# Feed-forward buffers of a streaming encoder layer at other starting addresses

## The chip, the cores and the metric

The kernel runs on one core of one Trainium2 chip. The metric is the device time of one execution in microseconds; the kernel before takes 2368.96 us, the median of three runs (2368.94 to 2370.51 us). A smaller time is better. All data is float32; the products run on TensorE in the fp32r form, each value split beforehand into a high and a low part.

## The reference, cut to what matters

One layer of an encoder is computed for a prompt of 2048 tokens and for 8 short samples of 16 tokens each, with `d_model` 1024. Written per token, with the states of the recurrent part left out:

```
q, k, v, gates, qa, ka, va = split(x @ w_in)            # 1024 -> 2824
hm = og * head_norm(mlstm(q, k, v, gates))              # 4 heads x 128
ha = swa(rope(qa), rope(ka), va)                        # 8 heads x 64
h  = layer_norm(alpha * x + concat(hm, ha) @ w_out)
u  = h @ w_up                                           # 1024 -> 2 * 2816
c  = b_conv + sum(ext(u)[j:j+T] * w_conv[j], j=0..2)    # over time, causal
a, g = split(c)
y  = layer_norm(alpha * h + (silu(g) * a) @ w_down)     # 2816 -> 1024
```

The outputs are `y` for the prompt and the samples, and the states that the next step needs. The change touches the lower half alone, the feed-forward (`w_up`, convolution, gate, `w_down`), and the end of the output projection by one pool.

## The kernel before, in words

Everything is done once, in stages that follow each other on TensorE without a pause: the input projection with the recurrent part and the attention woven into it, the output projection with its layer norm, the up-projection (`f_ups`), the down-projection (`f_downs`). The order of TensorE's instructions is that in which the program writes them; the tile framework adds the semaphores and lays out the memory.

The up-projection works in three blocks of tokens (`FBLOCKS`: 6, 6 and 5 tiles of 128 tokens). A block's normalised rows are transposed on TensorE into `hraw`, with the model dimension on the partitions. Products follow a seven-product scheme of Strassen's kind: for each of the 22 pairs of feature tiles `j`, seven sums of feature quarters (numbers `s` = 1 to 7) are multiplied with seven sums of weight quarters. A sum of features is split into a high part `hh` and a low part `hl` (`f_tokens`, `split` at L217 and L218), once per block; a sum of weights is split into one buffer `uw`, high half and low half one behind the other (`f_next`). One product `(b, j, s)` is twelve matmuls (`f_product`, L1831): four slices of the contraction, and for each of them high by high, high by low, low by high:

```
for k in range(4):
    for i, (l, r) in enumerate(((wh, hh), (wh, hl), (wl, hh))):
        mm(ps, l[:, k], r[:, k], ...)
```

The first operand `l`, here the weights, is loaded into the array (the stationary operand, a LDWEIGHTS in the profile); the second, `r`, here the features, is streamed through it (the moving operand, 384 columns in blocks 0 and 1, 320 in block 2). That is 22 x 7 x 12 = 1848 matmuls in each block. In the profile's rows the moving operand stands first: `dps<-hh,uw` is a product that writes the PSUM tile `dps`, streams `hh` and has `uw` loaded.

The down-projection uses the same scheme with the roles exchanged (L2034): the gated features `fu`, split into the six buffers that held `hh1` to `hl6`, are stationary, and the weights `uw` stream through, 512 columns at a time, in 1980 matmuls.

The output projection before them (`group`, by `mm3` at L222 to L224) also streams 512 columns of weights (`w`) past stationary features (`oh`, `ol`).

Memory is handed out by pools, which are stacks. A pool gives each tag its place in the order in which the tags first come; every tile takes its size rounded up to 32 bytes of a partition. A pool on the left begins where the one below it ends, and one on the right ends at the top and so begins lower when it gets larger. The starting addresses of the buffers in the program before, in bytes of a partition:

| buffers | pool | start | remainder by 256 |
|---|---|---|---|
| `uw`, `w`: 8 weight buffers, 4096 bytes in slots of 4224 | `wsb` | 17088 + 4224 i, 50368 + 4224 i | 192 and 64 in turn |
| `uw`: two spare weight buffers | `wx2sb` | 67584, 71680 | 0 |
| `w`: two spare weight buffers of the output projection | `wx1sb` | 141312, 145408 | 0 |
| `oh`, `ol` | `xsb` | 75776 + 4096 i | 0 |
| `hh`, `hl` of `s` = 2, 5, 3 | `f2sb` | 75776 + 6144 i | 0 |
| `hh`, `hl` of `s` = 4; `cc`, `th` | `f3sb` | 127520 and on | 32 |
| `hraw`, `hh` and `hl` of `s` = 1, 7, 6, all `fu` | `fsb` | 159712 and on | 224 |

The slices that a matmul reads lie whole multiples of 512 bytes behind these starts, so that the remainder by 256 of a buffer is that of each of its slices. The ten weight buffers `uw` are taken in turn (`f_slot`, `self.slot` modulo 10: eight of `wsb`, then two of `wx2sb`). The weights for a product are begun six to eight products ahead of it (`AHEAD`).

## Time and profile before

| what | value |
|---|---|
| median of three runs | 2368.96 us |
| span of the profiled execution (first to last instruction) | 2366.3 us |
| what lies around the span, against the median | 2.66 us |
| TensorE busy | 2318.5 us, 98% |
| VectorE, ScalarE, GpSimd busy | 77%, 54%, 12% |
| mean granted TensorE clock | 0.994 |
| TensorE's matmuls of the up-projection | 937.6 to 1881.2 us |
| TensorE's matmuls of the down-projection | 1883.1 to 2358 us |

The profiled execution's own time is its span and the time around it; the profile gives the span alone, and the median is 2.66 us above it. A matmul's row shows how long one was under way (0.34 us for 384 columns), but matmuls follow one another before the last has ended; what a matmul costs the program is the distance from its start to the next one's start, which is called its pitch from here on.

### The profile page before, as it was taken

The page shows a single profiled execution, that of the slowest core. Times are in us where ns is not written, and L with a number is a line of the kernel's source. Part 1 is how long each engine was busy: PE and PEld are TensorE (multiplying, and loading weights), DVE is VectorE, ACT ScalarE, POOL GpSimd, SP SyncE. Part 2 cuts the span into 40 slices and gives each one's busy share as a digit, 9 for nine tenths or more (in the row PEclk, how much of TensorE's full clock was granted, in tenths as well). Part 3 has the DMA queues.
Part 4 walks back from the last instruction along what each step waited for, and adds up shares of the span by engine and source line. Part 5 has one row for each costly group of instructions (what it writes and reads, how often), then busy time and mean ns, then how long its engine had stood idle before and what let it go on. Part 6 is the DMA issues. An engine that isn't in the chain of part 4 may idle for free.

```text
span 2366.3 us, 39878 instructions
## 1 busy us (share of the span) xinstructions
PE 2318.5 (98%) x14425; PEld 2122.9 (90%) x14425; DVE 1828.0 (77%) x3180; ACT 1282.8 (54%) x2423; POOL 281.7 (12%) x322
## 2 busy tenths in 40 slices
PE   8999999999999999999999999999999999999998
PEld 8999998998987777999999999999999978778776
DVE  8677587796689888987888776778766786895987
ACT  5353466776765565555556455555544544444543
POOL 0101101101112121200000000002100100300400
PEclk8999999999999999999999999999999999999999
DMA  7788889889976667787777899878998776657753
GB/s 276 268 302 298 289 284 324 282 288 328 301 256 224 228 208 254 279 309 281 280 270 254 308 310 318 307 247 291 320 276 258 218 280 218 232 175 222 229 167 107
DMA packets 296933, 624.98 MB, mean 264 GB/s; under 512 B 47004, under 2 KB 140192, under 8 KB 296736
## 3 DMA queue, kind: packets, MB, share of 16 engines
q1 hardware_dynamic: 294144, 612.99, 76.5%
q0 software_dynamic: 1728, 6.29, 0.7%
q10 hardware_dynamic: 864, 3.15, 0.4%
q8 instruction: 114, 1.87, 0.3%
q14 instruction: 83, 0.68, 0.1%
HBM read 451.78 MB, written 170.56 MB: 263 GB/s over the span
## 4 chain that ended last, share of the span: by engine, by line
PE 67%; DVE 9%; issue 4%; ACT 2%; DMA 2%; POOL 1%; SPq 0%; DVEq 0%; POOLq 0%; ACTq 0%
PE dps L1831 18%; PE fup L1831 18%; PE fht L2034 5%; PE dps L2034 5%; PE dps L700 5%; PE fup L2034 4%; PE dps L222 2%; PE dps L224 2%; PE dps L223 2%; PE ppo L1337 1%; DVE uw L218 1%; DVE w L218 1%; PE psc L1288 1%; PE dps L726 1%; DVE hl L218 1%
## 5 line engine op out<-in xcount | busy, mean ns | idle before, releaser
L1831 PE MATMUL dps<-hh,uw 128*128 128x384 f32 (+1 forms) x1848 | 481.3, 329 | 6.7 <-ACT u L1856 1.9
L1831 PE MATMUL fup<-hh,uw 128*128 128x384 f32 (+1 forms) x1848 | 480.3, 328 | 2.4 <-ACT u L1856 2.2
L1831 PEld LDWEIGHTS dps<-hh,uw 128*128 128x128 f32 x1848 | 330.0, 188 | 10.2 <-ACT u L1856 2.7
L1879 DVE SCALAR_TENSOR_TENSOR cc<-u,cw,cc 128x768 f32<-128x768 f32 (+1 forms) x264 | 252.4, 977 | 107.2 <-ACT cc L1877 105.3
L1831 PEld LDWEIGHTS fup<-hh,uw 128*128 128x128 f32 x1848 | 330.2, 188 | 3.7 <-ACT u L1856 3.1
L1831 PE MATMUL fup<-hl,uw 128*128 128x384 f32 (+1 forms) x924 | 302.9, 328 | 1.7 <-DVE hl L218 1.7
L1831 PE MATMUL dps<-hl,uw 128*128 128x384 f32 (+1 forms) x924 | 302.5, 327 | 0.0
L700 PE MATMUL dps<-w,oh 128*128 128x256 f32 x1344 | 257.9, 286 | 3.4 <-ACT zev L767 1.9
L218 DVE TENSOR_TENSOR w<-wraw,w 128x1024 fp32r<-128x1024 f32 (+2 forms) x167 | 190.5, 1148 | 60.7 <-ACT w L217 60.0
L217 ACT CAST w<-wraw 128x1024 fp32r<-128x1024 f32 (+2 forms) x167 | 163.1, 986 | 124.4 <-PE dps L700 49.4
L217 ACT CAST uw<-wraw 128x1024 fp32r<-128x1024 f32 x126 | 122.9, 977 | 195.7 <-PE dps L2034 99.3
L700 PEld LDWEIGHTS dps<-w,oh 128*128 128x128 f32 x1344 | 212.9, 190 | 15.6 <-issue 8.9
L218 DVE TENSOR_TENSOR uw<-wraw,uw 128x1024 fp32r<-128x1024 f32 x126 | 150.6, 1197 | 62.6 <-ACT uw L217 62.4
L1877 ACT ACTIVATE cc<-u,cw 128x768 f32<-128x768 f32 (+1 forms) x132 | 129.6, 998 | 117.2 <-DVE u L1870 59.5
L700 PE MATMUL dps<-w,ol 128*128 128x256 f32 x672 | 188.9, 281 | 0.0
L2034 PE MATMUL fup<-uw,fu 128*128 128x512 f32 x726 | 176.6, 399 | 9.4 <-ACT fht L2041 6.9
L2034 PEld LDWEIGHTS fup<-uw,fu 128*128 128x128 f32 x726 | 136.9, 189 | 44.4 <-ACT fht L2041 7.8
L1831 PEld LDWEIGHTS fup<-hl,uw 128*128 128x128 f32 x924 | 173.5, 188 | 2.5 <-DVE hl L218 2.5
L700 PE MATMUL dps<-oh,w 128*128 128x256 f32 x896 | 169.4, 284 | 5.9 <-ACT dps L775 2.8
L1831 PEld LDWEIGHTS dps<-hl,uw 128*128 128x128 f32 x924 | 173.6, 188 | 0.0
L2034 PE MATMUL dps<-uw,fu 128*128 128x512 f32 x660 | 165.0, 395 | 0.0
L700 PEld LDWEIGHTS dps<-oh,w 128*128 128x128 f32 x896 | 141.4, 190 | 12.2 <-issue 4.1
(328 smaller groups left out, 4661.3 us busy)
## 6 DMA issues: line engine op xcount, KB each, us to landing
uw<-zw SPq DMA_DIRECT2D x176, 512.0 KB, 4.7
zw<-uw SPq DMA_DIRECT2D x88, 512.0 KB, 3.0
w<-zws SPq DMA_DIRECT2D x72, 512.0 KB, 6.4
wv<-wup SPq DMA_DIRECT2D x66, 512.0 KB, 5.8
wraw<-wi SPq DMA_DIRECT2D x65, 512.0 KB, 5.2
wraw<-zt SPq DMA_DIRECT2D x60, 512.0 KB, 4.3
wraw<-wdn SPq DMA_DIRECT2D x45, 512.0 KB, 4.0
wraw<-wo SPq DMA_DIRECT2D x40, 512.0 KB, 4.7
```

Source lines behind the costliest of these rows:

```text
L217: nc.scalar.copy(hi, src)
L218: nc.vector.tensor_sub(lo, src, hi.bitcast(F32))
L222: mm(out, ah, bh, start=start, stop=False)
L223: mm(out, ah, bl, start=False, stop=False)
L224: mm(out, al, bh, start=False, stop=stop)
L700: mm(o, l, r, start=s in (1, 7) and c == k == i == 0, stop=k == 3 and i == 2, skip_group_check=True)
L726: mm(o, x, w, start=k == i == 0, stop=k == KD - 1 and i == 2, skip_group_check=True)
L1288: nc.tensor.matmul(ps[kvh][:, j, :nk], q[rs, j0 + j], k[rs, sel], start=i == 0, stop=i == 2)
L1831: mm(ps, l[:, k], r[:, k], start=s in (1, 7) and k == 0 and i == 0, stop=k == 3 and i == 2, skip_group_check=True)
L1877: S.activation(c[:, v], u[:, v, 2:2 + n], AF.Identity, bias=w[3], scale=w[2])
L1879: V.scalar_tensor_tensor(c[:, v], u[:, v, i:i + n], w[i], c[:, v], op0=ALU.mult, op1=ALU.add)
L2034: mm(ps, l[:, k, c], r[:, k], start=s in (1, 4, 7) and u == 0 and k == 0 and i == 0, stop=u == nu - 1 and k == n - 1 and i == 2, skip_grou ...
```

## The change: the buffers' starts

A helper `skew(pool, n)` takes a tile of `n` bytes that nothing reads or writes. It is called at five places:

- 480 bytes at the end of `fsb`, a pool on the right: all of its buffers move 480 bytes down, and `hraw`, `hh`, `hl` of `s` = 1, 7, 6 and `fu` have the remainder 0 by 256 (159232 for `hraw`).
- 64 bytes at the start of `wx1sb` and of `wx2sb`: the spare weight buffers have the remainder 64; `osb` behind `wx1sb` moves by 64 too.
- 448 bytes at the end of `wx2sb`: with the 64 it moves `f2sb`, and later `dsb`, by 512, so that their remainders stay.
- 480 bytes at the end of `f2sb`: `f3sb` moves by 992, from 121888 to 122880, and `hh`, `hl` of `s` = 4, `cc` and `th` have the remainder 0.

The buffers of `wsb`, `xsb` and the input stage stay. No instruction is added, removed or moved.

```diff
+    def skew(self, pool, n):
+        pool.tile([P, n // 4], F32, name="skew", tag=f"skew{n}", bufs=1)
+
...
             wx, wxcm = enter("wx1sb")
+            self.skew(wx, 64)
             self.unit_more(wx)
...
             self.wx, wxcm = enter("wx2sb")
+            self.skew(self.wx, 64)
             self.f2, f2cm = enter("f2sb")
             self.f3, f3cm = enter("f3sb")
             self.f_ups(n)
+            self.skew(self.f2, 480)
+            self.skew(self.wx, 448)
             close(f3cm)
...
             ln2.append(t)
+        self.skew(self.fp, 480)
         self.in_down = True
```

## The prediction, before the result was known

> **What bounds the kernel now.** I read the page's first parts, then the waits of TensorE, the chain of work that ended last, and last the single matmuls in order of time. From the page:

> ```profile
> span 2366.3 us, 39878 instructions
> PE 2318.5 (98%) x14425; PEld 2122.9 (90%) x14425; DVE 1828.0 (77%) x3180; ACT 1282.8 (54%) x2423; POOL 281.7 (12%) x322
> ...
> uw<-zw SPq DMA_DIRECT2D x176, 512.0 KB, 4.7
> ```

> TensorE is the bound. What it waited for from the start of the up-projection to the end (columns: total us, times, longest):

> ```profile
> PE fup L2034 <- ACT fht L2041: 6.9, 2, 3.5
> PE fup L1831 <- ACT u L1856: 2.2, 3, 1.1
> ...
> PE fht L2034 <- DVE yacc L2063: 0.2, 1, 0.2
> ```

> The list has eleven rows, 19.8 us in all; none names a DMA. So in the 1430 us that the change touches nothing but the pitch of the matmuls carries time. The chain of waits (start, length, count) gives it directly, as its pieces there are runs of matmuls that wait for nothing:

> ```profile
> 1020.38 6.25 PE dps L1831 x36
> 1217.77 6.32 PE fup L1831 x36
> 1796.04 5.29 PE dps L1831 x36
> 2265.01 15.40 PE dps L2034 x66
> 2345.47 6.31 PE fht L2034 x27
> ```

> That is 173.6 and 175.6 ns for 384 columns, 146.9 for 320, and 233.3 and 233.7 for 512. Two runs of the same 36 instructions in the up-projection differ by 2 ns a matmul, and neither has a wait in it. Since the instructions are alike, I looked at which buffers they read.

> **Does the pitch depend on addresses?** The timeline of TensorE shows it product by product. The rows below are the first low-part matmul of ten products in turn (all of 384 columns), so that two neighbours lie twelve matmuls apart:

> ```profile
> 1159.11 0.34 PE L1831 MATMUL fup<-hl,uw 128*128 128x384 f32 x1
> 1161.23 0.34 PE L1831 MATMUL fup<-hl,uw 128*128 128x384 f32 x1
> 1163.31 0.34 PE L1831 MATMUL fup<-hl,uw 128*128 128x384 f32 x1
> 1165.40 0.34 PE L1831 MATMUL dps<-hl,uw 128*128 128x384 f32 x1
> 1167.49 0.33 PE L1831 MATMUL fup<-hl,uw 128*128 128x384 f32 x1
> 1169.58 0.34 PE L1831 MATMUL dps<-hl,uw 128*128 128x384 f32 x1
> 1171.67 0.34 PE L1831 MATMUL fup<-hl,uw 128*128 128x384 f32 x1
> 1173.79 0.34 PE L1831 MATMUL dps<-hl,uw 128*128 128x384 f32 x1
> 1175.88 0.34 PE L1831 MATMUL dps<-hl,uw 128*128 128x384 f32 x1
> 1177.95 0.34 PE L1831 MATMUL dps<-hl,uw 128*128 128x384 f32 x1
> ```

> By the order in the code these are `s` = 6, 2, 5 of j = 14, `s` = 1 of j = 15, 3, 7, 4, then 6, 2, 5 of j = 15. Write a product as (remainder by 256 of the streamed features, of the loaded weights). Then (224, 192), the first, takes 2.12 us; (0, 192) 2.08; (0, 64), (224, 64), (0, 64), (224, 64) 2.09 each; (32, 0) 2.12; (224, 0) 2.09; (0, 192) 2.07. So 172.5 to 176.7 ns a matmul, and the same pair gives the same time.

> Over all starts of a stage I sorted the pitches by the pair (streamed operand, operand that is loaded next), leaving out matmuls beside other work and those that hold a wait (here a pitch above 200 ns; 173, 253 and 147 ns for the 320, 512 and 256 columns below). The up-projection's stretch of 384 columns has 3696 matmuls, of which 3628 stay; first and last row:

> ```profile
> 937.61 0.43 PE L1831 MATMUL fup<-hh,uw 128*128 128x384 f32 x1
> ...
> 1607.99 0.34 PE L1831 MATMUL dps<-hh,uw 128*128 128x384 f32 x1
> ```

> Mean pitch in ns (count): (0, 0) 174.91 (302); (0, 64) 174.85 (617); (0, 192) 173.15 (625); (224, 0) 174.22 (305); (224, 64) 174.39 (615); (224, 192) 176.40 (639); (32, 0) 176.78 (107); (32, 64) 174.17 (213); (32, 192) 176.40 (205). The standard errors are 0.07 to 0.21 ns. Products take the weight buffers in turn, so a pair isn't tied to one `s` or one minute of the run.

> **The change part by part.** No instruction, DMA or queue entry goes, comes or moves; every term is a count of matmuls by a difference of pitches.

> *Up-projection, `s` = 1, 7, 6 in blocks 0 and 1* (3 x 44 x 12 = 1584 matmuls): features from 224 to 0, spare weights from 0 to 64. Weighted by the counts, the three cells of 224 average 175.18 ns. Afterwards (0, 64) holds the 920 of the first two and (0, 192) the 639 of the third: 174.15. The price of those pairs is measured, since `s` = 2, 5, 3 have them already. 1.03 ns x 1584 = 1.6 us less.

> *`s` = 4* (528 matmuls): from 32 to 0: 175.57 to 174.19, 0.7 us less. *`s` = 2, 5, 3*: only (0, 0) becomes (0, 64), nothing.

> *Block 2, 320 columns* (1848 matmuls):

> ```profile
> 1598.47 0.31 PE L1831 MATMUL fup<-hh,uw 128*128 128x320 f32 x1
> ...
> 1881.20 0.31 PE L1831 MATMUL dps<-hh,uw 128*128 128x320 f32 x1
> ```

> All nine pairs lie between 146.45 and 146.94 ns; the same sum gives 0.2 us less. Up-projection together: 2.6 us less.

> *Down-projection* (1980 matmuls): the stationary features go from 224 to 0, a fifth of the streamed weights from 0 to 64. First and last row, and 233.28 ns is the mean of 1958 pitches:

> ```profile
> 1883.05 0.95 PE L2034 MATMUL fup<-uw,fu 128*128 128x512 f32 x3
> ...
> 2356.73 1.33 PE L2034 MATMUL fht<-uw,fu 128*128 128x512 f32 x5
> ```

> Now: (0, 224) 232.60 (393), (64, 224) 234.11 (785), (192, 224) 232.80 (780). The pairs that come, (64, 0) for 60% and (192, 0) for 40%, aren't in this stage. They are in the output projection, which streams 512 columns from the same weight buffers past features with the remainder 0:

> ```profile
> 651.04 0.40 PE L222 MATMUL dps<-w,oh 128*128 128x512 f32 x1
> ...
> 928.06 0.39 PE L223 MATMUL dps<-w,oh 128*128 128x512 f32 x1
> ...
> 936.33 0.39 PE L223 MATMUL dps<-w,oh 128*128 128x512 f32 x1
> ```

> Its last 36 matmuls take 8.27 us from the second row to the third, 229.7 ns each. Over the stage, with 816 matmuls, 669 pitches lie between 200 and 260 ns: (0, 0) 230.16 (134), (64, 0) 230.58 (276), (192, 0) 232.58 (259). 0.6 x 230.58 + 0.4 x 232.58 = 231.38: 1.90 ns below 233.28, times 1980 is 3.8 us less. Bounds: at best all of it falls to that stage's best pair, 230.16, which is 6.2 us less. At worst, the input projection's cells, same weight pairs at 256 columns: 3360 matmuls from

> ```profile
> 21.69 0.28 PE L700 MATMUL dps<-oh,w 128*128 128x256 f32 x1
> ...
> 642.80 0.28 PE L700 MATMUL dps<-w,oh 128*128 128x256 f32 x1
> ```

> There (64, 0) is 117.87 (921) and (192, 0) 116.04 (915), mean 116.96; doubled for 512 columns 233.9, 0.6 above today's, 1.2 us more. I take 3.8, by the rows of equal width and equal pairs.

> *Output projection*: its two spare buffers go from (0, 0) to (64, 0); a fifth of 816 by 0.42 is 0.1 us more.

> *VectorE and ScalarE* read and write the moved buffers. I cost this at nothing:

> ```profile
> L218 DVE TENSOR_TENSOR uw<-wv,uw 128x512 fp32r<-128x512 f32 x132 | 90.6, 686 | 49.7 <-ACT uw L217 49.6
> ```

> By weight buffer the means of this group are 685.7 to 686.5 ns for the five remainders by 512, and TensorE covers them: without cover a whole split of 0.69 us is at stake once, not a part of it. *DMAs*: the spare buffers' loads land in 4.7 us (the page's row above) and are issued at least six products of 2.1 us ahead, 12.6 us; they would have to more than double before TensorE waits. *New overlaps in memory*: `hl2`, `hl5`, `hl3` and the second spare buffer reach into one more old buffer of the output projection each. TensorE waits there today, for `hl2`:

> ```profile
> 941.66 0.68 DVE L1608 SCALAR_TENSOR_TENSOR ymix<-ymix,dps 128x512 f32<-128x512 f32 x1
> ...
> 944.06 1.75 DVE L218 TENSOR_TENSOR hl<-hraw,hh 128x1536 fp32r<-128x1536 f32 x1
> ...
> 945.87 0.44 PE L1831 MATMUL fup<-hl,uw 128*128 128x384 f32 x1 [1.51 <-DVE hl L218]
> ```

> L1608 is the last reader of the old buffers, on VectorE itself, and ends at 942.34, before `hl2` is begun in the same queue; so nothing is added. If ScalarE, which waits for the same reader, were held longer by one of its casts, the 1.5 us could about double.

> Sum: 2.6 + 3.8 - 0.1 = 6.3 us less. Against the profiled execution, span 2366.3 to 2360.0; the median of the runs lies 2.66 us above the span, 2368.96 to 2362.7, which is 0.27%. With the bounds of the down-projection, 2360.2 to 2367.7.

> [...]

> **The rivals.**

> 1. *The up-projection alone gains.* The output projection's lower pitch could come from its surroundings instead (VectorE and ScalarE do other things there), and the down-projection stays at 233.3. For it: the input projection's 233.9. Against: equal width and weights in the output projection. 2368.96 - 2.6 = 2366.4.
> 2. *Addresses only look like the cause*, no pitch changes: 2369.0. For it: block 2 shows no dependence at all. Against: the repeated times of equal pairs.
> 3. *Slower: a streamed start at 64 or 192 past stationary features at 0.* In the input projection these cells lie 2.21 ns above the cells with the roles exchanged, (0, 64) 114.51 (604) and (0, 192) 114.99 (614). If that came on top in the down-projection, twice for twice the columns, 4.4 ns x 1980 is 8.7 us more, less the 2.6: 2375.1. It decides from a pitch of 237.0 ns (2.6 + 4.7 us over 1980) in the down-projection. Against: the output projection's (64, 0) and (192, 0), both below 232.6.

> **How the numbers follow.** The forecast has 0.57, rival 1 0.24, rival 2 0.10, rival 3 0.07, and 0.02 is left for more than the best bound. A measurement of this kernel tells about 0.2%, 4.7 us, from no change. A small part of the forecast's share ends above 2364.2 and counts as the same: faster 0.55, same 0.37, slower 0.08. The range takes the best bound and some 0.7 us for the runs' spread below, and rival 2 above: 2359.5 to 2369.6; it leaves out rival 3 and the edges. The likeliest case alone has 2360.2 to 2365.

> **What the changed profile would show.** Chain pieces of 66 matmuls of the down-projection 15.27 us long rather than 15.40; products of `s` = 6 on weights at 192 at 2.08 us rather than 2.12; triples of 36 in blocks 0 and 1 none above 6.29; block 2 still 5.28; the output projection as before; VectorE's and ScalarE's groups and TensorE's list of waits unchanged. The prediction is wrong if the down-projection's pitch stays at 233 or rises, if products on buffers with the remainder 0 differ from today's, or if TensorE's waits grow, at the stage's first products above all.

## The result

The changed kernel takes 2364.59 us, the median of 15 runs (2360.43 to 2370.63), beside 2369.82 us of the kernel before in as many runs on the same chip (2363.58 to 2375.79). The ratio is 0.9976, with a 95% interval of 0.9969 to 0.9983: 0.24% faster, where 0.27% was forecast (2362.7 us; the time lies inside the range). Measured once more on another chip the ratio was 0.9973 (0.9962 to 0.9983; 2364.70 us in 8 runs beside 2371.31 in 24).

The head of the page after the change, with the product groups of the down-projection:

```profile
span 2361.2 us, 39878 instructions
PE 2312.4 (98%) x14425; PEld 2121.3 (90%) x14425; DVE 1829.6 (77%) x3180; ACT 1282.7 (54%) x2423; POOL 268.9 (11%) x322
...
L2042 PE MATMUL fup<-uw,fu 128*128 128x512 f32 x726 | 176.2, 399 | 10.6 <-ACT fht L2049 7.4
...
L2042 PE MATMUL dps<-uw,fu 128*128 128x512 f32 x660 | 163.2, 393 | 0.0
uw<-zw SPq DMA_DIRECT2D x176, 512.0 KB, 4.6
```

The counts of instructions are those of before. The lines have moved (L1831 to L1838, L2034 to L2042, L217 and L218 to L220 and L221, L2041 to L2049, L2063 to L2071). VectorE's and ScalarE's busy times stayed within 1.6 us, and TensorE's fell by 6.1 us. The profiled execution took 2362.99 us with a span of 2361.2, so 1.8 us lie around it.

The pieces of the chain of waits (start, length, count), which answer to those quoted of before:

```profile
958.88 6.45 PE dps L1838 x36
...
1201.17 6.29 PE dps L1838 x36
...
1793.40 5.28 PE dps L1838 x36
...
2260.81 15.22 PE dps L2042 x66
2276.03 14.56 PE fht L2042 x63
2314.11 15.26 PE dps L2042 x66
```

The same 66 matmuls of the down-projection took 15.40 us before and take 15.22 to 15.26 now; 63 took 14.71 and take 14.56. In the up-projection the pieces of 36 that reached 6.31 to 6.36 are gone, and block 2 is at 5.28 as it was. The first piece (6.45; 6.48 before) had been overlooked in the prediction's "none above 6.29": it is the longest in both kernels, whatever the addresses.

Over all matmuls, sorted as in the prediction (mean pitch in ns, by the remainders of the streamed operand and of the one that is loaded next):

| stage | before | pairs now | after | forecast |
|---|---|---|---|---|
| up-projection, 384 columns (3696) | 174.81 | (0, 64) 174.69, (0, 192) 173.25 | 174.10 | 174.85 and 173.15 for the two pairs |
| up-projection, 320 columns (1848) | 146.72 | (0, 64), (0, 192) | 146.56 | 0.1 lower |
| down-projection, 512 columns (1980) | 233.28 | (64, 0) 229.49, (192, 0) 232.54 | 230.71 | 231.38, from 230.58 and 232.58 |
| output projection, 512 columns (816) | 231.27 | (64, 0) 230.32, (192, 0) 232.40 | 231.13 | 0.1 higher |

Count times pitch falls from 917.2 to 914.4 us in the up-projection and from 461.9 to 456.8 us in the down-projection, 7.9 us together. TensorE's waits in the down-projection (total us, times, longest), first those of before that stand behind the 6.9 us for `fht`, then those of after:

```profile
PE fup L2034 <- DVE uw L218: 1.6, 1, 1.6
PE fup L2034 <- DVE yacc L2063: 0.9, 2, 0.5
PE fht L2034 <- DVE yacc L2063: 0.2, 1, 0.2
```

```profile
PE fup L2042 <- ACT fht L2049: 7.4, 2, 3.7
PE fup L2042 <- DVE uw L221: 1.7, 1, 1.7
PE fup L2042 <- DVE yacc L2071: 1.5, 2, 0.8
PE fht L2042 <- DVE yacc L2071: 0.2, 1, 0.2
```

Together they grew from 9.6 to 10.8 us. One stretch shows how: from the start behind a wait for `yacc` to the start behind the next wait for `fht` it is 24.03 us in both kernels (2050.19 to 2074.22 us before, 2046.01 to 2070.04 now). The 87 matmuls between them take 0.24 us less, and the wait behind them is 0.24 us longer (3.71 after 3.47). In the repeat of the changed kernel on another chip the waits add to 10.7 us.

### The profile page after: what moved, and what is told of

Read it like the earlier page. It is cut to its first block, busy times and chain, and to the rows that moved or that the text cites. A ratio compares the mean times of both kernels' runs of the same rounds, so it can differ in the third digit from the quotient of the medians.

```text
span 2361.2 us, 39878 instructions
## 1 busy us (share of the span) xinstructions
PE 2312.4 (98%) x14425; PEld 2121.3 (90%) x14425; DVE 1829.6 (77%) x3180; ACT 1282.7 (54%) x2423; POOL 268.9 (11%) x322
## 3 DMA queue, kind: packets, MB, share of 16 engines
q0 software_dynamic: 1728, 6.29, 0.8%
## 4 chain that ended last, share of the span: by engine, by line
PE 62%; DVE 13%; DMA 5%; ACT 4%; issue 3%; POOL 1%; SPq 0%; DVEq 0%; ACTq 0%; POOLq 0%
PE dps L1838 15%; PE fup L1838 15%; PE dps L707 7%; PE fht L2042 5%; PE dps L2042 5%; PE fup L2042 3%; DMA zf<-cc 2%; DVE cc L1886 2%; PE dps L225 1%; DVE uw L221 1%; PE dps L227 1%; PE dps L226 1%; PE ppo L1344 1%; ACT cc L1884 1%; DVE w L221 1%
## 5 line engine op out<-in xcount | busy, mean ns | idle before, releaser
L1838 PE MATMUL dps<-hh,uw 128*128 128x384 f32 (+1 forms) x1848 | 480.5, 328 | 7.0 <-ACT u L1863 1.9
L1838 PE MATMUL fup<-hh,uw 128*128 128x384 f32 (+1 forms) x1848 | 479.1, 328 | 2.7 <-ACT u L1863 2.5
L1838 PEld LDWEIGHTS dps<-hh,uw 128*128 128x128 f32 x1848 | 329.7, 188 | 11.0 <-ACT u L1863 3.1
L1838 PEld LDWEIGHTS fup<-hh,uw 128*128 128x128 f32 x1848 | 329.8, 188 | 3.9 <-ACT u L1863 3.4
L1838 PE MATMUL fup<-hl,uw 128*128 128x384 f32 (+1 forms) x924 | 302.3, 327 | 0.2 <-DVE hl L221 0.2
L1838 PE MATMUL dps<-hl,uw 128*128 128x384 f32 (+1 forms) x924 | 302.0, 327 | 0.0
L221 DVE TENSOR_TENSOR w<-wraw,w 128x1024 fp32r<-128x1024 f32 (+2 forms) x167 | 190.4, 1148 | 57.0 <-ACT w L220 54.6
L220 ACT CAST w<-wraw 128x1024 fp32r<-128x1024 f32 (+2 forms) x167 | 163.0, 985 | 124.0 <-PE dps L707 44.0
L220 ACT CAST uw<-wraw 128x1024 fp32r<-128x1024 f32 x126 | 122.8, 977 | 192.3 <-PE dps L2042 97.4
L221 DVE TENSOR_TENSOR uw<-wraw,uw 128x1024 fp32r<-128x1024 f32 x126 | 150.6, 1197 | 60.0 <-ACT uw L220 59.5
L2042 PE MATMUL fup<-uw,fu 128*128 128x512 f32 x726 | 176.2, 399 | 10.6 <-ACT fht L2049 7.4
L2042 PEld LDWEIGHTS fup<-uw,fu 128*128 128x128 f32 x726 | 138.0, 191 | 44.1 <-ACT fht L2049 8.2
L1838 PEld LDWEIGHTS fup<-hl,uw 128*128 128x128 f32 x924 | 173.4, 188 | 1.0 <-DVE hl L221 1.0
L1838 PEld LDWEIGHTS dps<-hl,uw 128*128 128x128 f32 x924 | 173.4, 188 | 0.0
L2042 PE MATMUL dps<-uw,fu 128*128 128x512 f32 x660 | 163.2, 393 | 0.0
L707 PEld LDWEIGHTS dps<-oh,w 128*128 128x128 f32 x896 | 141.7, 191 | 13.6 <-issue 4.1
## 6 DMA issues: line engine op xcount, KB each, us to landing
uw<-zw SPq DMA_DIRECT2D x176, 512.0 KB, 4.6
zw<-uw SPq DMA_DIRECT2D x88, 512.0 KB, 2.9
w<-zws SPq DMA_DIRECT2D x72, 512.0 KB, 6.2
wv<-wup SPq DMA_DIRECT2D x66, 512.0 KB, 5.6
wraw<-wi SPq DMA_DIRECT2D x65, 512.0 KB, 5.5
wraw<-zt SPq DMA_DIRECT2D x60, 512.0 KB, 4.3
wraw<-wdn SPq DMA_DIRECT2D x45, 512.0 KB, 4.1
wraw<-wo SPq DMA_DIRECT2D x40, 512.0 KB, 4.9
```

What stands on the lines that cost most here:

```text
L220: nc.scalar.copy(hi, src)
L221: nc.vector.tensor_sub(lo, src, hi.bitcast(F32))
L707: mm(o, l, r, start=s in (1, 7) and c == k == i == 0, stop=k == 3 and i == 2, skip_group_check=True)
L1838: mm(ps, l[:, k], r[:, k], start=s in (1, 7) and k == 0 and i == 0, stop=k == 3 and i == 2, skip_group_check=True)
L2042: mm(ps, l[:, k, c], r[:, k], start=s in (1, 4, 7) and u == 0 and k == 0 and i == 0, stop=u == nu - 1 and k == n - 1 and i == 2, skip_grou ...
```

## The experiments

The theory: what a matmul costs depends on where its streamed operand and the loaded operand begin, and the pitches of the pairs carry the gain. The main rival: the addresses only go along with something else (the work beside it, the order, the block), and any of the new layouts could have brought the same.

**Every pair of remainders, with nothing beside it.** TensorE alone runs series of 24 matmuls from two big tiles, for all 64 pairs of starts in steps of 32 bytes and for four widths:

```
for n in (384, 512, 256, 320):
    for r in range(0, 256, 32):          # start of the streamed operand
        for q in range(0, 256, 32):      # start of the loaded operand
            for i in range(24):
                mm(ps[:, :n], view(sta, q, ...), view(mov, r, ...), ...)
```

> This kernel leaves the whole computation out and writes zeros; TensorE alone runs 24 matmuls for each of 8 x 8 pairs of remainders by 256 bytes (streamed operand, loaded operand) in steps of 32 bytes, at 384, 512, 256 and 320 columns, with no other engine or DMA beside it for most of the time; behind them stand series in which two remainders of the loaded operand alternate. Address theory: the pitch depends on the pair as in the large kernel, at 384 columns (0, 192) near 173.2 ns, (0, 64) near 174.7, (224, 192) and (32, 0) near 176.5; at 512 columns (64, 0) near 229.5, (192, 0) near 232.5, (64, 224) near 234.1; at 320 all pairs within 0.5 ns. In the alternating series the pitch follows the remainder that is loaded next. Rival (the surroundings: other engines' reads and writes at the same time make the differences): no difference over 0.5 ns between the pairs of one width.

Five of its stretches at 512 columns, as a table of windows (window and its length, then busy time and count for TensorE, its weight load, VectorE and GpSimd, the granted clock, DMA share, GB/s). Each reaches from the first start of a pair to that of the next; 24 matmuls start inside, and the count takes in one or two that overlap the edge:

```profile
304.25:309.70 5.45, 5.45 (x25) 4.51 (x25) 0.00 (x0) 0.00 (x0) 1.00 0.00 0
315.30:320.90 5.60, 5.60 (x26) 4.51 (x24) 0.00 (x0) 0.00 (x0) 1.00 0.00 0
337.71:343.21 5.50, 5.50 (x25) 4.51 (x24) 0.00 (x0) 0.00 (x0) 1.00 0.00 0
393.40:398.90 5.50, 5.50 (x25) 4.51 (x24) 0.00 (x0) 0.00 (x0) 1.00 0.00 0
571.57:577.16 5.59, 5.59 (x25) 4.49 (x24) 0.00 (x0) 0.00 (x0) 1.00 0.00 0
```

They are (0, 0), (0, 64), (0, 192), (64, 0) and (192, 0). The granted clock is 1.00 in each, no other engine works, the instruction is the same, and still 24 matmuls take 5.45 to 5.60 us. (0, 192) equals (64, 0), and (0, 64) equals (192, 0): over the whole table, a few cells aside, the pitch follows the difference of the two starts by 256. Typical pitches in ns by that difference (streamed minus loaded):

| columns | 0 | 32 | 64 | 96 | 128 | 160 | 192 | 224 |
|---|---|---|---|---|---|---|---|---|
| 384 | 173.8 | 176.6 | 173.3 | 176.6 | 176.2 | 173.3 | 174.7 | 173.3 |
| 512 | 226.7 | 233.3 | 228.9 | 233.3 | 233.3 | 234.1 | 233.4 | 233.2 |

At 320 columns all 64 pairs lie between 146.6 and 146.9; at 256 most lie between 117 and 120, without so clear a rule. Cells stray: (32, 0) at 384 columns has 173.3, where its difference has 176.6 elsewhere. In further series the loaded operand changed with every matmul. With 512 columns, streamed at 0 and loaded at 64 and 192 in turn, the pitch before the load at 192 was 228.8 and that before the load at 64 was 232.7, as if the next load counted; the other series do not divide so cleanly (loaded at 0 and 64 in turn: 229.0 and 230.6, whose sum is that of the two pairs, 460). At 384 columns, streamed at 0, loads at 64 and 192 in turn gave 176.0 and 177.0, both above the prices of the two pairs (174.7 and 173.3), so where the starts alternate the prices of pairs need not add up. That it is the next load and not the own one that counts is suggested, not shown.

This is the rule behind the cells of the prediction: the streamed features at 224 past weights at 192 differ by 32 (176.6 here, 176.40 in the kernel before), and 0 past 192 by 64 (173.3 and 173.15). It also gives the down-projection's terms: 0.6 x 228.8 + 0.4 x 233.3 = 230.6 ns after, 233.3 before.

**One part of the change at a time.** First the 480 bytes of `fsb` alone:

```diff
         ln2.append(t)
+        self.skew(self.fp, 480)
         self.in_down = True
```

> Only the 480 bytes in the pool of hraw, hh/hl of s = 1, 7, 6 and fu. Address theory: in the up-projection these products go from 175.2 to 174.2 ns (1.6 us less), s = 4 keeps 175.6; in the down-projection (0, 0) near 230.2, (64, 0) near 229.5, (192, 0) near 232.5, mean 230.8 against 233.3 (4.9 us less). Together 6.5 us less pitch, so a ratio of 0.9972 to 0.9985, as good as the whole change or nearly. Rival (the spare buffers' move or f3sb carries the gain): ratio 1.000.

2364.07 us (11 runs) beside 2371.28, a ratio of 0.9972 (0.9963 to 0.9981). The down-projection's pitch is 230.67, the up-projection's 174.16: this one line carries the whole change, within the measurement.

Then the 480 bytes of `f2sb` alone, which move `hh` and `hl` of `s` = 4:

```diff
             self.f_ups(n)
+            self.skew(self.f2, 480)
             close(f3cm)
```

> Only the 480 bytes at the end of f2sb, so that hh/hl of s = 4, cc and th begin at a remainder of 0. Address theory: products of s = 4 at 384 columns go from 175.6 to 174.2 ns, 0.7 us less in all, nothing else changes: the down-projection's mean stays at 233.3. Rival (cc and th matter, by VectorE and ScalarE): VectorE's groups on cc and th get faster than 977 and 957 ns.

One run: 2369.61 us beside 2371.28. The up-projection's pitch falls to 174.53, the down-projection's stays at 233.29. The term forecast as 0.7 us comes to 0.9 by count times pitch (917.2 to 916.3); a single time can't show it. VectorE's groups on `cc` and `th` take 978 and 920 ns, where they took 977 and 919, so the other explanation, that these two buffers matter, falls.

Then the spare weight buffers alone:

```diff
             wx, wxcm = enter("wx1sb")
+            self.skew(wx, 64)
...
             self.wx, wxcm = enter("wx2sb")
+            self.skew(self.wx, 64)
...
             self.f_ups(n)
+            self.skew(self.wx, 448)
```

> Only the 64 bytes before the spare weight buffers, and the 448 behind them. Address theory: no gain; in the down-projection the pair (0, 224) at 232.6 ns becomes (64, 224) at 234.1 for a fifth of the matmuls, 0.6 us more, in the up-projection (32, 0) at 176.8 becomes (32, 64) at 174.2 for a fifth of s = 4, 0.3 us less. Rival (the spare buffers at 0 were what cost time): 2 us less or more.

One run: 2372.55 us. The pitches are 174.74 and 233.40, so nothing by itself, as (0, 224) gave way to (64, 224). The pieces of the same 66 matmuls, in the chains of these three kernels in turn:

```profile
2263.19 15.21 PE dps L2038 x66
```

```profile
2266.51 15.40 PE dps L2038 x66
```

```profile
2269.40 15.41 PE dps L2040 x66
```

Only the first has the shorter piece.

**The same features at 0, but bad partners.** If the features' start at 0 were what helps, it would help past any weights. Here the features' buffers keep their remainders (the spare buffers' pool has its unused tiles at 192 and 64 bytes instead of 64 and 448), and the weights are written into their slots at other offsets, so that the up-projection has (0, 128) and (0, 224) and the down-projection (160, 0) and (224, 0):

```diff
-            return self.wp.tile([P, KD, P], dt, name="uw", ...)
-        return self.wx.tile([P, KD, P], dt, name="uw", ...)
+            near = self.slot in (0, 1, 3, 4)
+            t = self.wp.tile([P, KD * P + 32], dt, name="uw", ...)
+            o = (8 if near else 24) if down else (8 if near else 16)
+        else:
+            t = self.wx.tile([P, KD * P + 64], dt, name="uw", ...)
+            o = 8
+        return t[:, o:o + KD * P].rearrange("p (a b) -> p a b", a=KD)
```

> The buffers of the changed kernel, but each weight buffer is read at a shift inside its slot, so that the up-projection has only the pairs (0, 128) and (0, 224) and the down-projection (160, 0) and (224, 0): features all at the remainder 0, and pairs that the pair experiment has as slow. Address theory, by its cells: 176.4 ns at 384 columns against 174.1 (8.5 us more), 0.4 x 234.1 + 0.6 x 232.8 = 233.3 against 230.7 in the down-projection (5.2 us more): 13.7 us more than the changed kernel, a ratio to the kernel before of 1.0035. Rival (it is the features' own start on a multiple of 256 that gains): as the changed kernel, 0.997 to 0.998.

2372.43 us (11 runs) beside 2369.32 (35 runs); the ratio is 1.0007 (0.9998 to 1.0016). All the gain is gone and the down-projection is back at 233.24 ns ((160, 0) 233.09, (224, 0) 233.33): the pair decides, not the features' start. It isn't as slow as was expected, since in the up-projection (0, 224) came to 175.01 ns and not to the 176.6 that had been put down for it ((0, 128) 176.04). By the table above (0, 224) differs by 32 and should have 176.6. Sorted product by product (the mean of the third to the eleventh matmul, products with a wait left out), this pair has two values in this run and nearly nothing between: 89 products lie at 173.2 ns on average and 93 at 176.6, where those of (0, 128) all lie between 175.3 and 176.4. So one pair can settle at two prices; the stray cell (32, 0) of the table, 173.3 where its difference has 176.6, looks like the same. What picks the price, no run shows.

**Better partners.** The other way round, all products of the up-projection at (0, 192), and the down-projection at (0, 0) for 60% and (64, 0) for 40% (the same edit with other offsets):

```diff
+            o = (16 if near else 0) if down else (0 if near else 32)
+        else:
+            o = 16 if down else 0
```

> The same shifts set to the fast pairs: the up-projection has (0, 192) alone, the down-projection (0, 0) for 60% and (64, 0) for 40%. Address theory: 173.25 ns at 384 columns against 174.1 (3.2 us less), 0.6 x 228.3 + 0.4 x 229.9 = 228.9 ns against 230.7 (3.5 us less): 6.7 us less than the changed kernel, a ratio to the kernel before of 0.995. Rival (features alone): as the changed kernel, 0.997 to 0.998.

2364.78 us (12 runs), a ratio of 0.9974 (0.9964 to 0.9984): no faster than the changed kernel, where 0.995 had been expected. Yet the pitches did fall, to 173.31 and 230.21 ns, 3.8 us less by count times pitch. The 173.31 is the price of TensorE alone (173.3), with all other engines at work. The 230.21 is not the 228.9 that was expected, and (0, 0) came to 229.99, where TensorE alone has 226.7. Sorting the pitches by the buffers shows where the 1.3 ns lie: a product of the down-projection streams a high and a low half of the weights, from two buffers. Where both halves begin alike, the means are 228.15 (both at 0) and 229.74 ns (both at 64), which at 60 and 40% make 228.8. Where one half begins at 0 and the other at 64, which is so in two products of five, the means are 232.06 and 233.01, above both, in the same stage and beside the same work. In the kernel with bad partners a mixture was cheaper instead: 231.18 for high halves at 224 and low ones at 160, where halves alike take 233.41 and 233.92. So a pair's price is best trusted for products that keep to one pair. No experiment took the mixtures apart, and why products with both halves at 0 take 228.15 ns and not 226.7 stays open.

So where did 3.8 us go? Part may have gone into the clock. In the down-projection of this profile TensorE was granted half its clock for 13.7 us, in the profile of before for 3.4, and in the two profiles of the changed kernel for 6.8 and 13.7, so single profiles don't decide it; the means over all runs, below, put it at 2.1 us. Such stretches stand in the trace of every whole kernel (the mean granted clock of these profiles is 0.991 to 0.997), and those of the down-projection lie in or right behind pauses of TensorE: in the profile of before from 2239.91 us, in a pause of 3.43 us that ends at 2240.21, and in the first of the changed kernel from 2069.47, in a pause that ends at 2070.04, and from 2236.72, behind one that ends at 2236.03. Two windows of the repeat of the changed kernel, ahead of its pause from 2067.3 to 2071.4 us and across the end of it (columns as above, with ScalarE ahead of GpSimd):

```profile
2062.00:2066.00 4.00, 4.00 (x19) 3.29 (x18) 4.00 (x3) 1.32 (x2) 3.68 (x3) 1.00 0.46 148
...
2070.00:2073.40 3.40, 1.99 (x5) 1.60 (x6) 3.40 (x4) 3.40 (x6) 1.51 (x1) 0.50 0.97 334
```

Here TensorE, which had been running at full clock (1.00), waits 3.73 us for ScalarE's copy (L2049) and then goes on at half the clock (0.50). Three further experiments go after the pause and the clock.

**The evacuation ahead of the norm.** The changed kernel, with the loop that evacuates the products moved ahead of the steps of the layer norm, in the hope of a shorter wait:

```diff
-            for f in pending[:2]:
-                if next(f, self) is self:
-                    pending.remove(f)
             if u == nu - 1 and not last:
                 for p in cols[::-1] if s == 7 else cols:
                     after(s, p)
+            for f in pending[:2]:
+                if next(f, self) is self:
+                    pending.remove(f)
```

> The changed kernel, and in the down-projection the evacuation of a finished product is issued ahead of the pending layer norm steps. Theory: the two waits of 3.7 to 4.1 us at the starts of a product (ScalarE's copy fht stands behind a layer norm step that waits for GpSimd) go, 6 us less; and the stretches of 3.4 us at half the granted clock that follow them at 2069 and 2236 us go too, as they follow a pause, 3.4 us less: ratio 0.994 to 0.996. Rival (the half clock has nothing to do with the pause): as many such stretches as before, and 6 us less at most. Rival (the copies wait for something else): no change against 0.9976.

2369.76 us (11 runs), ratio 1.0001 (0.9991 to 1.0011), where 0.994 to 0.996 had been expected: the gain of the change is lost. TensorE's waits in its down-projection:

```profile
PE fup L2042 <- ACT fht L2049: 4.9, 2, 2.5
PE dps L2042 <- DVE uw L221: 4.0, 1, 4.0
PE fup L2042 <- DVE yacc L2071: 3.6, 2, 1.9
PE fup L2042 <- DVE uw L221: 1.7, 1, 1.7
PE fup L2042 <- DVE yacc L2069: 0.9, 1, 0.9
PE fht L2042 <- DVE yacc L2071: 0.2, 1, 0.2
```

The two waits for ScalarE fell from 7.4 to 4.9 us, but those for `yacc` rose by 3.0, and a new one of 4.0 came for the split of the weights on VectorE, which now stands behind the evacuation. The order was a better balance than it looked.

**Both.** The better partners with this order:

> Both together, the fast pairs and the changed order. If the terms add: 6.7 and 6 to 9 us less than the changed kernel, 2349 to 2352 us, a ratio to the kernel before of 0.991 to 0.9925. If the shorter pitch only makes the waits longer: 0.994 to 0.995.

2368.72 us (11 runs), ratio 0.9992 (0.9983 to 1.0001): 3.9 us slower than with the better partners alone, and neither of the two times that had been expected.

**Which pause brings the half clock?** TensorE alone again: series of 60 matmuls of 512 columns, and between two series n dependent steps of VectorE that it must wait for:

```
for n in (0, 1, 2, 3, 4, 5, 6, 8):
    for rep in range(8):
        for i in range(60):
            matmul(ps, sta, mov, ...)
        t = copy(ps)                      # n steps on VectorE
        for j in range(n - 1):
            t = t + raw
        sta = t - t                       # the next series needs it
```

> The whole computation is left out and the outputs are written with zeros. TensorE runs series of 60 matmuls of 512 columns with the same two operands; between two series it waits for a chain of n dependent VectorE steps, eight series for each of n = 0, 1, 2, 3, 4, 5, 6, 8. In the whole kernels a stretch of 3.4 us with the granted clock at one half, and a matmul pitch of 426 ns, follows several of TensorE's pauses of 2 to 4 us. Theory (a pause of TensorE itself brings the half clock): no such stretch for n = 0 and for pauses well under 2 us, and one or more of 3.4 us (some 8 matmuls at 426 ns) behind pauses from some length between 2 and 4 us on. Rival (the stretches belong to something else in the whole kernels, to the work beside TensorE or to DMAs): none in any series behind the start of the run.

Rows of its timeline (start, length, the run of matmuls, the pause ahead of it):

```profile
129.72 13.89 PE L260 MATMUL run<-mov,next 128*128 128x512 f32 x60 [1.20 <-DVE next L270]
...
250.58 15.50 PE L260 MATMUL run<-mov,next 128*128 128x512 f32 x60 [1.83 <-DVE next L270]
267.92 13.90 PE L260 MATMUL run<-mov,next 128*128 128x512 f32 x60 [1.83 <-DVE next L270]
...
668.34 16.61 PE L260 MATMUL run<-mov,next 128*128 128x512 f32 x60 [4.01 <-DVE next L270]
```

and the windows of the series with pauses of 1.1, 1.8, 2.6, 3.3, 4.0 and 4.7 us, in turn, with the granted clock in the column after the engines' counts:

```profile
129.00:248.00 119.00, 110.52 (x478) 89.20 (x479) 7.42 (x16) 0.00 (x0) 1.00 0.00 1
250.00:385.00 135.00, 120.92 (x480) 96.35 (x480) 12.84 (x24) 0.00 (x0) 0.92 0.00 0
386.00:523.00 137.00, 117.16 (x480) 93.78 (x480) 18.32 (x32) 0.00 (x0) 0.95 0.00 0
525.00:666.00 141.00, 116.03 (x480) 92.89 (x480) 23.21 (x39) 0.00 (x0) 0.96 0.00 0
668.00:830.00 162.00, 131.98 (x480) 104.79 (x480) 28.02 (x46) 0.00 (x0) 0.83 0.00 0
833.00:995.00 162.00, 126.72 (x480) 100.84 (x480) 33.06 (x53) 0.00 (x0) 0.85 0.00 0
```

A series takes 13.9 us at full clock. Behind pauses of 1.1 us none of the 8 was longer (clock 1.00); behind 1.8 us 6 of 8 had a stretch of 3.41 us at half clock (15.5 us); behind 2.6 and 3.3 us 4 and 3 of 8; behind 4.0 us all 8, and for 6.8 us each (16.5 us); behind 4.7 us all 8 again, seven of them for 6.8 us. So a pause of TensorE is enough, with nothing beside it but VectorE's short steps, and a short pause, where it is hit, costs 1.6 us on top of itself, one of 4 us 2.6. Of pauses of one length, 1.8, 2.6 or 3.3 us, some were hit and some not. The starts of all 37 stretches lie on one grid of 3.413 us, as do those in the traces of the whole kernels (within 3 ns in the profiles of before and of the changed kernel), so it may go by when the pause comes; that is a reading of these starts, and no run set the moment of a pause.

**The pauses filled.** In the changed kernel, 34 matmuls on the identity ahead of the first product of `s` = 2 in blocks 1 and 2 of the down-projection, where the two waits for ScalarE lie, and the same in the kernel with the better partners, with the changed kernel once more beside them:

```diff
+            if b and s == 2 and u == 0:
+                for i in range(34):
+                    mm(banks[3][:, :P], self.ident, self.ident, start=i == 0, stop=i == 33, ...)
```

> The changed kernel once more, as the measure on this chip for the two kernels sent with it. Both theories: a ratio of 0.997 to 0.9985 to the kernel before.

> The changed kernel with 34 matmuls of 128 columns on the identity matrix added ahead of the first product of s = 2 in token blocks 1 and 2 of the down-projection, into a PSUM bank that is free there. TensorE waits there about 4.1 us for the evacuation of the products before; the added matmuls take some 34 x 0.06 = 2.2 us or more of that wait and are not needed by anything. Theory (the pause of about 4 us brings a stretch of 3.4 us at half the clock behind it, which costs 1.7 us each time): no half-clock stretch behind these two places, and a time up to 3.4 us below that of the changed kernel, 2361 to 2364 us; never more than 1 us above it. Rival (the stretches have another cause): the stretches stay, and the time is that of the changed kernel or a little above it.

> The same filling in the kernel whose weight views sit at remainder 192 in the up-projection and 0 and 64 in the down-projection. Its pitches are worth 3.8 us more than the changed kernel's by count times mean, of which the time showed nothing, since its waits at product starts and half-clock stretches took 6 us. Theory (half-clock stretches took it): with the pauses filled it comes to 2358 to 2362 us, 2 to 4 us below the filled kernel with the changed kernel's pairs. Rival (the gain of a faster TensorE goes into the waits for the evacuation, whatever the clock does): within 1.5 us of that kernel.

The changed kernel took 2364.70 us, the filled one 2370.84 (ratio 0.9997, 0.9986 to 1.0008), the filled one with better partners 2366.59 (0.9983, 0.9974 to 0.9992). The filled one at the first place, in its timeline, and the windows there:

```profile
2066.82 7.75 PE L2096 MATMUL dps<-ident 128*128 128x128 f32 x68
2074.33 6.01 PE L2042 MATMUL fup<-uw,fu 128*128 128x512 f32 x25
```

```profile
2070.00:2073.40 3.40, 3.40 (x32) 3.40 (x32) 3.40 (x3) 3.40 (x7) 2.22 (x1) 1.00 0.63 214
```

The half clock is gone there and at the other place; in the whole down-projection of this profile none is left, where the unfilled kernel beside it has 13.7 us of it. But the filling was mis-sized: each of the 34 matmuls stands in the profile as two, and they take 7.5 us (68 rows at 0.110 us) where 2.2 had been estimated (34 at 0.06 us, a quarter of the 230.7 ns of 512 columns), more than the 4.1 us, from start to start, that they were to fill. So the time went up. The first half of the theory (the stretches follow the pause) holds; its times, 2361 to 2364 us and 2358 to 2362 us with the better partners, do not, and a filling of the right size wasn't run.

**Time at full clock.** Each run lists its mean granted clock c, so time x (1 - c) is what was taken off its clock, TensorE's idle moments included, and time x c what it would take at full clock if all of that counted; means over all runs of a kernel, in us (standard errors of the last column 0.4 to 0.8; each c is rounded to 0.001, which is 2.4 us of one run):

| kernel (runs) | mean time | taken by the clock | at full clock |
|---|---|---|---|
| before, on the chip of the repeat and the filled ones (24) | 2371.3 | 13.4 | 2357.9 |
| before, on the chip of both partners and of the other order (35) | 2370.3 | 12.3 | 2358.0 |
| changed, first chip (15) | 2364.8 | 13.6 | 2351.2 |
| changed, again (8) | 2365.0 | 13.3 | 2351.7 |
| bad partners (11) | 2372.3 | 11.6 | 2360.7 |
| better partners (12) | 2364.6 | 15.6 | 2349.0 |
| changed, other order (11) | 2370.5 | 14.4 | 2356.1 |
| better partners, other order (11) | 2368.5 | 18.7 | 2349.7 |
| changed, filled (11) | 2370.5 | 10.8 | 2359.7 |
| better partners, filled (11) | 2367.1 | 10.3 | 2356.7 |

The change is worth 6.2 us at full clock (2357.9 to 2351.7, on one chip), and the clock takes as much as before. The kernel before has the same time at full clock on both chips, so the rows of different chips can be compared in the last column. The bad partners are 2.7 us slower than the kernel before, where their pitches say 2.1. The better partners gain 2.5 us more at full clock (against the mean of the two rows of the changed kernel, with a standard error of about 0.9) and lose 2.1 of it to the clock; where the pauses are filled, they keep theirs: 3.0 us at full clock, 3.5 in the mean time. That is the difference that the theory expected of the pair of filled kernels (2 to 4 us; the rival, within 1.5). The filling itself takes 2.6 us off the clock's share and adds 8.2 us of work and waits. The other order costs 4.6 us at full clock with the changed kernel's pairs and 0.7 with the better ones. In the profiles the waits of the down-projection grow with it from 10.8 to 15.3 us and from 11.0 to 13.9, which accounts for the first and not for the second; no run took that apart.

## Why the prediction was right, step by step

- *Pitch depends on the two starts.* Right, and shown with TensorE alone. Rival 2 (addresses only look like the cause) falls by the 5.45 and 5.60 us of one instruction that differs only in its operands' starts.
- *Up-projection, 2.6 us less.* It is 2.8 by count times pitch, with (0, 64) and (0, 192) at 174.69 and 173.25 where 174.85 and 173.15 had been taken. The product of `s` = 6 on weights at 192 now takes 2.08 us (was 2.12), from the second of these rows of the timeline (the first low-part matmuls of `s` = 4, 6 and 2) to the third, and `s` = 4 ahead of it 2.09:

```profile
1155.20 0.34 PE L1838 MATMUL dps<-hl,uw 128*128 128x384 f32 x1
...
1157.29 0.33 PE L1838 MATMUL fup<-hl,uw 128*128 128x384 f32 x1
...
1159.37 0.34 PE L1838 MATMUL fup<-hl,uw 128*128 128x384 f32 x1
```

- *Down-projection, 3.8 us less.* The mechanism was right and the size was not: 5.1 us. The price of (64, 0) was taken from the output projection as 230.58 and is 229.49 here, close to the 228.8 of TensorE alone; (192, 0) was taken as 232.58 and is 232.54. The same pair costs a nanosecond more in one stage than in the other, and the term carries 1980 matmuls; whether that comes from the mixed halves (in the changed kernel products with both halves at 64 take 229.37) or from the work beside them, no run took apart. It lies inside the bounds given. The upper of these has a slip: it takes the plain mean of its two cells, 116.96, where the forecast's own shares of 60 and 40% give 117.14, so that the bound is 2.0 us more and not 1.2. Rival 1 (the down-projection stays at 233.3) and rival 3 (it rises to 237.0 and more) fall by the 230.71.
- *Output projection, 0.1 us more.* 231.27 to 231.13 ns; too little to tell.
- *TensorE's waits unchanged.* This is the step that failed. The prediction let the gain of a faster TensorE come out whole, and priced the cover of VectorE's and ScalarE's work by the splits alone. Where the evacuation sets the pace, as in the stretch of 24.03 us, what TensorE gains goes into the wait: the waits grew from 9.6 to 10.8 us in the down-projection (10.7 in the repeat). In the up-projection the listed waits differ by more between two runs of the same program, 9.2 and 13.1 us, than before and after. So of 7.9 us by the pitches about 1.1 go into waits, 6.8 would be left, and 6.2 are measured at full clock (with a standard error of 0.9).
- *VectorE, ScalarE and the DMAs at nothing.* Right: the splits take 686 ns as before and the weights' loads, those of the spare buffers among them, land in 4.6 us (4.7). The wait for `hl2`, 1.5 us before and possibly twice that, was 0.2 us in the first profile and 1.5 in the repeat, so it goes by the run and not by the addresses.
- *The sum.* 6.3 us, made of a term too small by 1.3 and a wait left out of 1.1, came out at 5.2 in the medians of the first comparison, 6.6 in those of the second, and 6.2 at full clock. That it fits so well is owed in part to two errors that cancel.

## What to carry to other kernels

When two runs of the same matmuls differ in pitch without a wait, sort the pitches by the starts of the streamed and the loaded operand; here their difference by 256 was worth up to 2% at 384 columns and 3% at 512 with TensorE alone, and one unused tile of 480 bytes changed it without an instruction. Only fp32r operands and steps of 32 bytes were measured. Price a pair from a stage with the same width in which a product keeps to that pair, look apart at products whose two halves begin differently, and expect a nanosecond of error. Then look at where the faster engine waits next: what it gains shows up in part as a longer wait, and behind a pause the clock can take more again (in the series with TensorE alone 1.6 us behind a pause of 1.8 us that was hit, 2.6 behind each of 4.0 us).
